# Staging and splitting the weights of a seven-product matmul two quarters at a time

## The chip, the cores and the metric

The kernel runs on one core of one Trainium2 chip. The metric is the device time of one execution in microseconds, median of several. Before the change it is 1718.91 us (three runs, 1718.07 to 1722.91).

## The reference

Two layers of a hybrid decoder trunk on 512 tokens of width 2048, all in float32. Each layer normalises its input, projects it through one combined matrix `w_in`, feeds three groups of heads, and projects their concatenation through `w_out` into the residual stream:

```python
def _layer(x, norm_g, w_in, ...):
    proj = _rmsnorm(x, norm_g) @ w_in        # 2048 x 7696
    # split: conv h,b,c,g (512 each); stick-breaking q,k,v,g (1024 each);
    #        linear attention q,k (256 each), v,g (512 each), low-rank gate (16)
    y_conv = _short_conv(...) * silu(cv_g)
    y_sb   = _stick_breaking(rmsnorm(q), rmsnorm(k), v) * silu(sb_g)   # 8 heads of 128
    y_gla  = _rmsnorm(_gla(...)) * silu(gl_g)                          # 4 heads
    return x + concat(y_conv, y_sb, y_gla) @ w_out                     # 2048 x 2048
```

The stick-breaking weights of a query are, strictly causally, sigmoid(z) times the product of sigmoid(-z) over the later keys; the kernel forms them by a scan backwards over a row of scores.

## The kernel before

**Projections.** Both matrices are worked through in groups of 256 columns: 26 of `w_in` and 8 of `w_out` in each layer. A group's 2 MB of float32 weights are fetched into one of two staging tiles `st` (`fetch`, L343). Each element is split into a high and a low float16 part (`wh`, `wl`), after scaling by a power of two that comes from the sum of the squares. A product of two such numbers takes three float16 matmuls: high by high, high by low, low by high. The scale comes from two Square instructions on ACT, one for each half of the staging tile (`wmax`, L366), a reduction over partitions on POOL (L380) and five tiny instructions on DVE (`wscale`). An ordinary group is then split in two halves of 128x2048 (L435 on ACT, L442 on DVE) and multiplied by 192 matmuls of 256 columns or 96 of 512 (`project_toks`, L683 to L685; `project_cols`, L673 to L675), or by tokens (L814).

**Quick groups.** 25 of the 68 groups take seven block products instead of eight, in the manner of Strassen and Winograd (`project_quick`, L749). These are g, k and the second "conv h" of `w_in` in each layer (18), and three and four groups of `w_out`. The 2048x256 weights are seen as quarters: r is the parity of the 128-row tile, c the half of the columns; b11, b12, b21, b22 are strided views of the staging tile. Sums of the quarters give four more blocks. `wsums` (L471) makes the sums in place and splits all seven blocks, 128x1024 each: the high part on ACT (L485), the low part on DVE (L486). The sums are four additions on DVE for `w_out` (L492 to L498), or three on DVE (L506, L508, L511) and one accumulating DMA on POOL's queue (L503). Each of the three buffers of `wh` and `wl` takes two blocks (parts 0 and 1, 2 and 3, 4 and 5), a separate tile `w7h`, `w7l` the seventh. The matching sums of the left operand lie ready (`xsums`, `msums`).

Each product is 24 matmuls of 256 columns (L764) or 48 of 128 (L767). Seven products go into four accumulators in two PSUM banks: pa and pd in one, pb and pf in the other. Between them ACT and DVE take the values out (L778 to L792): y12 from pa after the first product, y21 from pb, y22 from pd, y11 from pa after the fifth, and so on. The products stand in the order pa w11, pb wT2, pd wT3, pf w22, pa w21, pb wt1, pd wT4. A matmul with `start` clears its bank's accumulation state, so only the first product in a bank has it.

**What sets the order.** DVE's and ACT's instructions are written out by hand only up to the first projection. From there on a planner orders the instructions of every engine: it runs the program on a timeline of its own, takes at each step what its operands allow, by priority, and inserts the semaphores. Each engine then executes its list strictly in that order. The preparation of weights has high priority. `weights()` (L515), called as a group starts, issues the fetch of the group after the next, and leaves two hooks: after the first three matmuls of the running group the squares of the next group are queued, and later (after the second product of a quick group, L779) its scaling and splits. A fetch waits until its staging tile's last reader is through; the fetches, the accumulating DMA and the POOL reductions share POOL's queue.

**Attention.** Each pair of heads j has four groups v, g, q, k, so quick and ordinary groups alternate. `attend` queues two `scores` and two `values`, which run beside the next pair's projections. `scores` (L1226 for the matmuls) computes the scores of four query tiles in two chunks, as `CHUNKS` (L40) lists them: tiles 3 and 2, then 0 and 1, with their column offsets in PSUM. Then come two sigmoids, a scan, a product, the split into float16 (L1244, L1245) and DMA transposes from SP's queue into `th`. The transposes of q and k (`qT`, `kT` from `qp`) go through the same queue. `values` multiplies by the values (L1263) into a single bank, whose two halves DVE evicts by two instructions (L1270).

Of the kernel before, what the change touches and what calls it, by code (L numbers as in the profile page):

```python
# [6 lines left out]
F16 = mybir.dt.float16  # L7
# [3 lines left out]
AF = mybir.ActivationFunctionType  # L11
ALU = mybir.AluOpType
# [5 lines left out]
P = 128  # L18
# [18 lines left out]
TWICE = ("wm", "wgm", "wq", "ws", "wp", "vu", "bm", "bsmix", "gsmix", "lr", "xr0", "xrm", "xrt", "xtot", "xrstd", "xrs")  # L37


CHUNKS = ((((3, 0), (2, 512)), (3, 2)), (((0, 0), (1, 128)), (0, 1)))  # L40


@with_exitstack
def hybrid_trunk(ctx, tc, x, norm_g, w_in, conv_w, conv_b, sb_qn_g, sb_kn_g,
# [7 lines left out]
    HK = KT // 2  # L52
# [18 lines left out]
    def nm(s):  # L71
        uid[0] += 1
        return f"{s}_{uid[0]}"
# [4 lines left out]
    def wk(shape, tag, bufs=None, dt=F32):  # L78
        return work.tile(shape, dt, tag=tag, name=nm(tag), bufs=bufs)
# [266 lines left out]
    def fetch(i):  # L346

        l, src, cols = specs[i]
        queue = nc.gpsimd if i > 2 else nc.sync
        staged[i] = st = []  # L350
        whole[i] = stage.tile([P, KT, GW], F32, tag="st", name=nm("st"))
        for h in range(2):
            s_ = whole[i][:, h * HK:(h + 1) * HK, :]
            c0 = cols[0][0]
            queue.dma_start(s_, src[l, h * HK * P:(h + 1) * HK * P, c0:c0 + GW].rearrange("(k p) n -> p k n", p=P))  # L355
# [110 lines left out]
    def hook(mm):  # L466

        if hooks:
            hooks.pop(0)(mm)

    def wsums(i):  # L471

        sc = scales[i]
        b11, b12, b21, b22 = (whole[i][:, r::2, c * P:(c + 1) * P] for r in range(2) for c in range(2))
        parts = loaded[i][0]
        for _ in range(3):
            a = [wpool.tile([P, HK, GX], F16, tag=t, name=nm(t)).rearrange("p k c -> p (k c)") for t in ("wh", "wl")]
            parts.extend([p_[:, n * HK * P:(n + 1) * HK * P] for p_ in a] for n in range(2))
        parts.append([wk([P, HK * P], t, 1, dt=F16) for t in ("w7h", "w7l")])
        for n in range(7):  # L480
            parts[n] = [a.rearrange("p (k c) -> p k c", c=P) for a in parts[n]]

        def split(b, n):
            h_, l_ = parts[n]
            hi = S.activation(h_, b, AF.Copy, scale=sc)  # L485
            V.scalar_tensor_tensor(l_, b, sc, h_, ALU.mult, ALU.subtract)  # L486
            return hi


        if specs[i][1] is w_out:  # L490
            split(b11, 0)
            V.tensor_tensor(b11, b11, b12, ALU.add)  # L492
            split(b22, 3)
            V.tensor_tensor(b12, b12, b22, ALU.add)
            V.tensor_tensor(b22, b11, b22, ALU.add)
            split(b22, 1)
            split(b12, 2)
            V.tensor_tensor(b22, b22, b21, ALU.add)  # L498
            split(b21, 4)
            split(b11, 5)  # L500
            split(b22, 6)
            return
        G.dma_start(out=b12, in_=b11, accum_op=ALU.add)  # L503
        split(b11, 0)
        split(b22, 3)
        V.tensor_tensor(b22, b12, b22, ALU.add)  # L506
        split(b22, 1)
        V.tensor_tensor(b11, b22, b11, ALU.subtract)  # L508
        split(b11, 2)
        split(b21, 4)  # L510
        V.tensor_tensor(b21, b22, b21, ALU.add)  # L511
        split(b12, 5)
        split(b21, 6)

    def weights():  # L515

        i = cursor[0]
        cursor[0] += 1
        if i + 2 < len(specs):
            with tc.high_priority():  # L520
                fetch(i + 2)
        assert not hooks
# [134 lines left out]
    for l in range(depth):  # L657
# [90 lines left out]

        def project_quick(src, sums, y, cols):  # L749

            (w11, wT2, wT3, w22, w21, wt1, wT4), u = weights()
            (pa, pd), (pb, pf) = ([bk[:, n * GW:(n + 1) * GW] for n in range(2)]
                                  for bk in [bank(psp, "p") for _ in range(2)])
            a11, a12, a22 = ([a[:, 2 * r:2 * r + 2, c::2, :] for a in src] for r, c in ((0, 0), (0, 1), (1, 1)))
            s_, a21_22, a12_s, a11_21 = sums

            def prod(o, w, a, start, stop=False):
                for t in range(1 if cols else 2):
                    for kk in range(HK):
                        for i, (p_, q_) in enumerate(((0, 0), (0, 1), (1, 0))):  # L760
                            st_ = start and t == kk == i == 0
                            en = stop and kk == HK - 1 and i == 2
                            if cols:
                                mm = T.matmul(o, w[q_][:, kk, :], a[p_][:, :, kk, :], start=st_, stop=en,  # L764
                                              skip_group_check=True)
                            else:
                                mm = T.matmul(o[:, t * P:(t + 1) * P], a[p_][:, t, kk, :], w[q_][:, kk, :], start=st_,  # L767
                                              stop=en, skip_group_check=True)
# [9 lines left out]
            S.activation(y12, za, AF.Copy)  # L778
            hook(prod(pb, wT2, s_, True))  # L779
            V.tensor_tensor(y21, zb, y12, ALU.subtract)  # L780
            prod(pd, wT3, a11_21, False)
            S.activation(y22, zd, AF.Copy)
            prod(pf, w22, a12_s, False)
            prod(pa, w21, a12, False)
            S.activation(y11, za, AF.Copy)
# [428 lines left out]
        def attend(j, qT, kT, vh, vl, vu, g, s_):  # L1214
# [34 lines left out]
            def values(hh):  # L1249
                hs = slice(hh * P, (hh + 1) * P)  # L1250
                op = bank(psm, "m").rearrange("p (t c) -> p t c", c=P)
                y = wk([P, NT, P], "e")
                for n, (qtiles, cols) in enumerate(CHUNKS):
                    at = {t: 7 * n + o // P for t, o in qtiles}
                    top, q0 = max(at), min(at)
                    for kt in range(top + 1):

                        ts_ = [t for t in cols if t >= kt]
                        first = at[ts_[0]] + kt
                        step = at[cols[1]] - at[cols[0]]  # L1260
                        c0 = 2 * n + cols.index(ts_[0])
                        for i, (a_, b_) in enumerate(((vh, 0), (vh, 1), (vl, 0))):
                            T.matmul(op[:, c0:c0 + len(ts_), :], a_[:, kt, hs],  # L1263
                                     th[hh][:, b_, first:first + (len(ts_) - 1) * step + 1:step, :],
                                     start=n == i == kt == 0, stop=n == 1 and i == 2 and kt == top,
                                     skip_group_check=True)
                for n, (_, cols) in enumerate(CHUNKS):
                    q0 = min(cols)
                    a = op[:, 2 * n:2 * n + 2, :]
                    V.scalar_tensor_tensor(y[:, q0:q0 + 2, :], a[:, ::-1, :] if cols[0] > cols[1] else a, vu[:, 1:2],  # L1270
                                           g[:, hh, q0 * P:(q0 + 2) * P].rearrange("p (t c) -> p t c", c=P),
                                           ALU.mult, ALU.mult)
# [158 lines left out]
```

## Time and profile before

| | |
|---|---|
| median of 3 runs | 1718.91 us |
| the profiled execution's own time | 1717.69 us |
| its span, first to last instruction | 1715.9 us |
| mean granted TensorE clock | 0.992 |
| PE, DVE, ACT, POOL busy | 97%, 78%, 66%, 14% of the span |
| DMA packets moved | 227.26 MB, mean 132 GB/s |

A row of a group reads: line, engine, operation, tile written <- tiles read, shapes, count | busy time in us, mean ns of one | idle time of the engine just before, and what ended most of it. "psp" are the PSUM banks of the projections, "st" the staging tiles, "m", "x" and "s" left operands and their sums. PE is TensorE's matmuls, PEld its weight loads, SP the queue of the transposes.

### The profile page before, as it was taken

The page shows a single profiled execution, that of the slowest core. Times are in us where ns is not written, and L with a number is a line of the kernel's source. Part 1 is how long each engine was busy: PE and PEld are TensorE (multiplying, and loading weights), DVE is VectorE, ACT ScalarE, POOL GpSimd, SP SyncE. Part 2 cuts the span into 40 slices and gives each one's busy share as a digit, 9 for nine tenths or more (in the row PEclk, how much of TensorE's full clock was granted, in tenths as well). Part 3 has the DMA queues.
Part 4 walks back from the last instruction along what each step waited for, and adds up shares of the span by engine and source line. Part 5 has one row for each costly group of instructions (what it writes and reads, how often), then busy time and mean ns, then how long its engine had stood idle before and what let it go on. Part 6 is the DMA issues. An engine that isn't in the chain of part 4 may idle for free.

```text
span 1715.9 us, 36876 instructions
## 1 busy us (share of the span) xinstructions
PE 1669.9 (97%) x15642; PEld 1298.4 (76%) x15642; DVE 1331.3 (78%) x2327; ACT 1129.1 (66%) x1619; POOL 239.2 (14%) x286
## 2 busy tenths in 40 slices
PE   7999999999999989999989999999999999899999
PEld 5644548989898964799976455689898889548998
DVE  8975889877878767785688677997786888677883
ACT  7667677767666656666665676776765767565662
POOL 1211111111111111001122101121111111101110
PEclk9999999999999999999999999999999999999999
DMA  7233323566766686245543332446666667753441
GB/s 251 83 114 98 99 64 99 145 116 152 136 149 139 147 233 164 77 150 181 186 103 108 116 102 75 118 123 125 148 136 105 146 132 150 201 153 108 162 151 50
DMA packets 181478, 227.26 MB, mean 132 GB/s; under 512 B 94194, under 2 KB 141628, under 8 KB 180800
## 3 DMA queue, kind: packets, MB, share of 16 engines
q0 software_dynamic: 60352, 168.83, 34.4%
q1 hardware_dynamic: 111952, 46.61, 14.4%
q10 hardware_dynamic: 9008, 9.45, 1.7%
q8 instruction: 122, 2.00, 0.5%
q14 instruction: 44, 0.36, 0.1%
HBM read 179.65 MB, written 14.68 MB: 113 GB/s over the span
## 4 chain that ended last, share of the span: by engine, by line
PE 73%; DVE 12%; DMA 7%; ACT 4%; issue 3%; POOL 0%; DVEq 0%; ACTq 0%
PE psp L767 13%; PE psp L674 8%; PE psp L675 8%; PE psp L673 8%; PE psp L685 7%; PE psp L684 7%; PE psp L683 7%; PE psp L814 6%; PE psp L764 3%; DMA st<-in_w_in_dram 2%; DVE wl L486 2%; DMA th<-za 2%; DMA kT<-qp 2%; ACT junk L366 1%; DVE wl L442 1%
## 5 line engine op out<-in xcount | busy, mean ns | idle before, releaser
L366 ACT ACTIVATE junk<-st 128x2048 uint8<-128x2048 f32 x150 | 285.1, 1901 | 44.1 <-DMA st<-in_w_in_dram 42.8
L442 DVE SCALAR_TENSOR_TENSOR wl<-st,ws,wh 128x2048 f16<-128x2048 f32 x102 | 239.2, 2347 | 80.7 <-ACT wh L435 80.7
L435 ACT ACTIVATE wh<-st,ws 128x2048 f16<-128x2048 f32 x100 | 199.3, 1998 | 105.4 <-PE psp L674 47.1
L684 PE MATMUL psp<-wl,m 128*128 128x256 f16 x960 | 261.7, 273 | 0.0
L683 PE MATMUL psp<-wh,m 128*128 128x256 f16 x960 | 261.7, 273 | 0.0
L685 PE MATMUL psp<-wh,m 128*128 128x256 f16 x960 | 261.7, 273 | 0.0
L485 ACT ACTIVATE wh<-st,ws 128x1024 f16<-128x1024 f32 x150 | 167.6, 1143 | 120.5 <-DVE st L506 57.7
L486 DVE SCALAR_TENSOR_TENSOR wl<-st,ws,wh 128x1024 f16<-128x1024 f32 x150 | 189.6, 1279 | 27.4 <-ACT wh L485 27.3
L355 POOL DMA_DIRECT2D st<-in_w_in_dram x114 | 102.2, 900 | 436.0 <-DVE wl L442 319.4
L683 PE MATMUL psp<-wh,x 128*128 128x256 f16 x512 | 139.6, 273 | 0.0
L684 PE MATMUL psp<-wl,x 128*128 128x256 f16 x512 | 139.6, 273 | 0.0
L685 PE MATMUL psp<-wh,x 128*128 128x256 f16 x512 | 139.6, 273 | 0.0
L675 PE MATMUL psp<-x,wl 128*128 128x512 f16 x352 | 134.4, 382 | 2.2 <-DVE zun L186 2.2
L674 PE MATMUL psp<-x,wh 128*128 128x512 f16 x352 | 134.4, 382 | 0.0
L673 PE MATMUL psp<-x,wh 128*128 128x512 f16 x352 | 134.0, 381 | 0.0
L673 PE MATMUL psp<-m,wh 128*128 128x512 f16 x352 | 133.9, 380 | 0.0
L674 PE MATMUL psp<-m,wh 128*128 128x512 f16 x352 | 133.9, 380 | 0.0
L675 PE MATMUL psp<-m,wl 128*128 128x512 f16 x352 | 133.9, 380 | 0.0
L675 PEld LDWEIGHTS <-wl 128*128 128x128 f16 x704 | 69.2, 98 | 85.0 <-DVE wl L442 2.7
L673 PEld LDWEIGHTS <-wh 128*128 128x128 f16 x704 | 69.2, 98 | 81.5 <-issue 3.1
L380 POOL PARTITION_ALL_REDUCE wgm<-wm x75 | 40.0, 533 | 648.2 <-ACT junk L366 633.6
L674 PEld LDWEIGHTS <-wh 128*128 128x128 f16 x704 | 69.2, 98 | 80.8 <-issue 2.3
(427 smaller groups left out, 4042.2 us busy)
## 6 DMA issues: line engine op xcount, KB each, us to landing
st<-in_w_in_dram POOLq DMA_DIRECT2D x114, 1024.0 KB, 8.4
st<-in_w_out_dram POOLq DMA_DIRECT2D x32, 1024.0 KB, 7.4
st<-st POOLq DMA_DIRECT2D x18, 512.0 KB, 8.3
st<-in_w_in_dram SPq DMA_DIRECT2D x6, 1024.0 KB, 12.0
mixd<-g POOLq DMA_DIRECT2D x24, 256.0 KB, 7.7
x<-in_x_dram SPq DMA_DIRECT2D x4, 1024.0 KB, 4.9
qT<-in_x_dram ACTq DMA_DIRECT2D x8, 512.0 KB, 3.8
qT<-xs ACTq DMA_DIRECT2D x8, 512.0 KB, 3.9
```

Source lines behind the costliest of these rows:

```text
L366: sq = S.activation(junk(HK * GW).rearrange("p (k n) -> p k n", k=HK), staged[i][h], AF.Square, accum_out=peak[i][:, h:h + 1])
L435: hi = S.activation(wh[:, :, :GW], staged[i][h], AF.Copy, scale=scales[i])
L442: V.scalar_tensor_tensor(wl[:, :, :GW], staged[i][h], scales[i], wh[:, :, :GW], ALU.mult, ALU.subtract)
L485: hi = S.activation(h_, b, AF.Copy, scale=sc)
L486: V.scalar_tensor_tensor(l_, b, sc, h_, ALU.mult, ALU.subtract)
L673: T.matmul(o, wh[:, kk, cs], xh[:, :, k, :], start=st_, stop=False)
L674: T.matmul(o, wh[:, kk, cs], xl[:, :, k, :], start=False, stop=False)
L675: mm = T.matmul(o, wl[:, kk, cs], xh[:, :, k, :], start=False, stop=en)
L683: T.matmul(o, ah[:, t, k, :], wh[:, kk, :n], start=st_, stop=False, skip_group_check=True)
L684: T.matmul(o, ah[:, t, k, :], wl[:, kk, :n], start=False, stop=False, skip_group_check=True)
L685: return T.matmul(o, al[:, t, k, :], wh[:, kk, :n], start=False, stop=en, skip_group_check=True)
L767: mm = T.matmul(o[:, t * P:(t + 1) * P], a[p_][:, t, kk, :], w[q_][:, kk, :], start=st_, stop=en, skip_group_check=True)
```

## The change

Three things are changed.

*Staging.* A quick group's weights are fetched by three DMAs instead of two, so that in each pair of row tiles the quarters lie side by side as b22, b11, b12, b21, 128 columns each. The first DMA brings b22 (512 KB in rows of 512 bytes), the second b11 and b12 (1 MB in rows of 1 KB), the third b21 (512 KB in rows of 512 bytes). The two Squares read columns 0 to 255 and 256 to 511 of that layout.

*Splits and products.* `wsums` splits b22 and b11 by one instruction on each engine, forms the sums in place, splits the two results by one, b12 and b21 by one, and the last sum alone. The same seven blocks come out, in the order w22, w11, wT2, wT3, wt1, w21, wT4. The sums of `w_out` groups are formed by the same formulas as those of `w_in`, with the first addition on DVE. The products now stand in the order pa w11, pf w22, pb wT2, pd wT3, pa w21, pb wt1, pd wT4, and the second hook stands after pf's product.

*Values.* The second chunk holds tile 1 at column 0 and tile 0 at column 256, so the four tiles lie in the bank in the order 3, 2, 1, 0, and one instruction of 128x512 evicts them, reading backwards by tiles.

```diff
-CHUNKS = ((((3, 0), (2, 512)), (3, 2)), (((0, 0), (1, 128)), (0, 1)))
+CHUNKS = ((((3, 0), (2, 512)), (3, 2)), (((1, 0), (0, 256)), (1, 0)))
...
+        if i in quick:
+            w = src[l, :, c0:c0 + GW].rearrange("(k r p) n -> p r k n", p=P, r=2)
+            own = whole[i].rearrange("p (k r) c -> p k (r c)", r=2)
+            for o, r, c in ((0, 1, slice(P, GW)), (P, 0, slice(0, GW)), (P + GW, 1, slice(0, P))):
+                queue.dma_start(own[:, :, o:o + c.stop - c.start], w[:, r, :, c])
+            st.extend(own[:, :, h * GW:(h + 1) * GW] for h in range(2))
+            return
...
+        own = whole[i].rearrange("p (k r) c -> p k (r c)", r=2)
+        b22, b11, b12, b21 = (own[:, :, n * P:(n + 1) * P] for n in range(4))
...
+        def split(src):
+            n = src.shape[2] // P
+            if n == 1:
+                pair = [wk([P, HK * P], t, 1, dt=F16) for t in ("w7h", "w7l")]
+            else:
+                pair = [wpool.tile([P, HK, GX], F16, tag=t, name=nm(t)).rearrange("p k c -> p (k c)")[:, :HK * n * P]
+                        for t in ("wh", "wl")]
+            h_, l_ = (a.rearrange("p (k c) -> p k c", c=n * P) for a in pair)
+            S.activation(h_, src, AF.Copy, scale=sc)
+            V.scalar_tensor_tensor(l_, src, sc, h_, ALU.mult, ALU.subtract)
+            parts.extend([a[:, :, m * P:(m + 1) * P] for a in (h_, l_)] for m in range(n))
...
         if specs[i][1] is w_out:
+            V.tensor_tensor(b12, b12, b11, ALU.add)
+        else:
+            G.dma_start(out=b12, in_=b11, accum_op=ALU.add)
+        split(own[:, :, :2 * P])
         V.tensor_tensor(b22, b12, b22, ALU.add)
-        split(b22, 1)
         V.tensor_tensor(b11, b22, b11, ALU.subtract)
-        split(b11, 2)
-        split(b21, 4)
+        split(own[:, :, :2 * P])
+        split(own[:, :, 2 * P:])
         V.tensor_tensor(b21, b22, b21, ALU.add)
-        split(b12, 5)
-        split(b21, 6)
+        split(b21)
...
-            (w11, wT2, wT3, w22, w21, wt1, wT4), u = weights()
+            (w22, w11, wT2, wT3, wt1, w21, wT4), u = weights()
...
-            hook(prod(pb, wT2, s_, True))
+            hook(prod(pf, w22, a12_s, True))
+            prod(pb, wT2, s_, False)
             V.tensor_tensor(y21, zb, y12, ALU.subtract)
             prod(pd, wT3, a11_21, False)
             S.activation(y22, zd, AF.Copy)
-            prod(pf, w22, a12_s, False)
             prod(pa, w21, a12, False)
...
-                for n, (_, cols) in enumerate(CHUNKS):
-                    q0 = min(cols)
-                    a = op[:, 2 * n:2 * n + 2, :]
-                    V.scalar_tensor_tensor(y[:, q0:q0 + 2, :], a[:, ::-1, :] if cols[0] > cols[1] else a, vu[:, 1:2],
-                                           g[:, hh, q0 * P:(q0 + 2) * P].rearrange("p (t c) -> p t c", c=P),
-                                           ALU.mult, ALU.mult)
+                V.scalar_tensor_tensor(y, op[:, ::-1, :], vu[:, 1:2], g[:, hh, :].rearrange("p (t c) -> p t c", c=P),
+                                       ALU.mult, ALU.mult)
```

More of the change, by code (lines that the diff above doesn't have):

```diff
@@ L351, in fetch @@
         whole[i] = stage.tile([P, KT, GW], F32, tag="st", name=nm("st"))
+        c0 = cols[0][0]
+        if i in quick:
[5 more added lines that the diff above has]
+            return
         for h in range(2):
             s_ = whole[i][:, h * HK:(h + 1) * HK, :]
-            c0 = cols[0][0]
             queue.dma_start(s_, src[l, h * HK * P:(h + 1) * HK * P, c0:c0 + GW].rearrange("(k p) n -> p k n", p=P))
@@ L473, in wsums @@
         sc = scales[i]
-        b11, b12, b21, b22 = (whole[i][:, r::2, c * P:(c + 1) * P] for r in range(2) for c in range(2))
+        own = whole[i].rearrange("p (k r) c -> p k (r c)", r=2)
+        b22, b11, b12, b21 = (own[:, :, n * P:(n + 1) * P] for n in range(4))
         parts = loaded[i][0]
-        for _ in range(3):
-            a = [wpool.tile([P, HK, GX], F16, tag=t, name=nm(t)).rearrange("p k c -> p (k c)") for t in ("wh", "wl")]
-            parts.extend([p_[:, n * HK * P:(n + 1) * HK * P] for p_ in a] for n in range(2))
@@ L479, in wsums @@
[L479 to L487, printed above, removed]
-        if specs[i][1] is w_out:
[L491 to L495, printed above, removed]
-            split(b22, 1)
-            split(b12, 2)
-            V.tensor_tensor(b22, b22, b21, ALU.add)
-            split(b21, 4)
-            split(b11, 5)
-            split(b22, 6)
-            return
@@ L503, in wsums @@
-        G.dma_start(out=b12, in_=b11, accum_op=ALU.add)
-        split(b11, 0)
-        split(b22, 3)
+        def split(src):
[9 more added lines that the diff above has]
+            parts.extend([a[:, :, m * P:(m + 1) * P] for a in (h_, l_)] for m in range(n))
```

2 lines of the change are left out of this document (removed).

## The prediction

> **What bounds the kernel now.** I read the page's head first, then the waits of TensorE, then the stages, then the lines that the diff touches.
>
> ```profile
> span 1715.9 us, 36876 instructions
> PE 1669.9 (97%) x15642; PEld 1298.4 (76%) x15642; DVE 1331.3 (78%) x2327; ACT 1129.1 (66%) x1619; POOL 239.2 (14%) x286
> PE 73%; DVE 12%; DMA 7%; ACT 4%; issue 3%; POOL 0%; DVEq 0%; ACTq 0%
> ```
>
> TensorE is busy 1669.9 of 1715.9 us, and the diff leaves its number of matmuls and their shapes as they are. So the change can win only where TensorE waits, and lose wherever it makes TensorE wait. The waits of PE, longest first (engine and line that waits, what ended it, us in total, times, longest):
>
> ```profile
> PE psz L1226 <- DMA kT<-qp: 11.0, 2, 5.9
> PE psp L764 <- ACT g L785: 5.5, 6, 1.9
> PE psp L814 <- DMA m<-raw: 4.9, 1, 4.9
> ...
> PE psm L1263 <- DVE e L1270: 3.6, 1, 3.6
> ...
> PE psp L767 <- DVE wl L486: 1.3, 1, 1.3
> ...
> PE psp L764 <- DVE wl L486: 1.0, 2, 0.6
> ...
> PE psp L764 <- ACT qT L778: 0.6, 2, 0.3
> ...
> PE psp L764 <- DVE g L780: 0.2, 1, 0.2
> ```
>
> What touches seven-product groups directly is 5.5 + 1.3 + 1.0 + 0.6 + 0.2 = 8.6 us, half a per cent of the run. Another 11.0 + 3.6 lie in attention stages which the engines that prepare weights make late. The 4.9 at L814 belongs to the change of layers and isn't touched. The stages (us, then busy time of PE, PEld, DVE, ACT, POOL, clock, DMA share, GB/s):
>
> ```profile
> 455.00:540.00 85.00, 84.73 (x945) 77.32 (x943) 69.97 (x125) 59.05 (x94) 14.41 (x16) 1.00 0.65 147
> 540.00:640.00 100.00, 92.96 (x970) 79.71 (x968) 77.10 (x136) 68.23 (x104) 16.59 (x19) 0.99 0.67 160
> 1300.00:1393.00 93.00, 87.40 (x946) 79.07 (x944) 69.85 (x125) 59.59 (x94) 14.39 (x16) 0.98 0.69 134
> 1393.00:1492.00 99.00, 91.82 (x963) 79.00 (x961) 76.99 (x136) 67.51 (x104) 16.55 (x19) 1.00 0.72 161
> 1616.00:1692.00 76.00, 76.00 (x1351) 75.63 (x1349) 62.84 (x82) 46.63 (x51) 6.94 (x10) 1.00 0.42 137
> ```
>
> The middle of a layer (455 to 540) and the last four quick groups (1616 to 1692) are full. The loss is in 540:640 and 1300:1492, some 20 us of PE, with DVE at 75 to 78% and DMA at two thirds.
>
> **Part 1, splitting two quarters at a time.** (us busy, mean ns. These count six parts of each of 25 groups; the seventh, w7, is as long.)
>
> ```profile
> L442 DVE SCALAR_TENSOR_TENSOR wl<-st,ws,wh 128x2048 f16<-128x2048 f32 x102 | 239.2, 2347 | 80.7 <-ACT wh L435 80.7
> L435 ACT ACTIVATE wh<-st,ws 128x2048 f16<-128x2048 f32 x100 | 199.3, 1998 | 105.4 <-PE psp L674 47.1
> L485 ACT ACTIVATE wh<-st,ws 128x1024 f16<-128x1024 f32 x150 | 167.6, 1143 | 120.5 <-DVE st L506 57.7
> L486 DVE SCALAR_TENSOR_TENSOR wl<-st,ws,wh 128x1024 f16<-128x1024 f32 x150 | 189.6, 1279 | 27.4 <-ACT wh L485 27.3
> ```
>
> Now a group takes seven splits: ACT 7 x 1.143 = 8.00 us, DVE 7 x 1.279 = 8.95. After it takes three of double width and one single: ACT 3 x 1.998 + 1.143 = 7.14, DVE 3 x 2.347 + 1.279 = 8.32. Over 25 groups that frees 21.6 us of ACT and 15.8 of DVE. Beside a full PE this is worth nothing by itself. What counts is the order: the first split now holds both untouched quarters, and products one and two read exactly these. The sums wait for one split instead of two in different buffers, and the third product's weights, late before (1.3 at L767, in the wait list), get a product more of slack. I take the 1.3 + 1.0 of weight waits as gone: **-2.3**. Bounds: -2.3 to +2.5, since each double split also delivers its first half up to 1.998 - 1.143 + 2.347 - 1.279 = 1.9 us later. That is covered by PE's work on the group before. The cover is short only where TensorE waited for L486 already, three places, so I set +2.5 as an estimate for the upper end.
>
> On the chain through 540:640 and 1393:1492 (DVE in a row, then the transposes of k) two quick groups are prepared in each stage. Each is shorter by 0.63 us of DVE, and I add as much again for hand-offs between the engines that go: 2 x 2 x 0.65 = **-2.6** off the 11.0. Bounds 0 (the DMA queue decides alone) and -11.0.
>
> **Part 2, the products in another order.** Two accumulators share a PSUM bank: pa with pd, pb with pf. How long is a product? From the chain of waits:
>
> ```profile
> 1300.37 5.24 PE psp L764 x48
> ```
>
> 48 matmuls of two products take 5.24, so a product is 2.6 us. And what does the next one in the same bank wait for? ACT's timeline (start, us, what):
>
> ```profile
> 387.79 1.91 ACT L366 ACTIVATE junk<-st 128x2048 uint8<-128x2048 f32 x1 [4.56 <-DMA st<-in_w_in_dram]
> 389.60 0.19 ACT L366 ACTIVATION_READ_ACCUMULATOR junk<-st 128x1 f32 x1
> 389.69 0.36 ACT L785 ACTIVATE g<-psp 128x256 f32<-128x256 f32 x1
> ```
>
> and TensorE's:
>
> ```profile
> 390.11 0.27 PE L764 MATMUL psp<-x,w7h 128*128 128x256 f16 x1 [1.06 <-ACT g L785]
> ```
>
> At 390.11 the seventh product, which writes pd, starts 0.06 us after L785 has read pa: other columns, same bank. Turns in a bank are therefore taken whole. Before, pa, pd, pa, pd stood one product apart each time. After, the order is pa, pf, pb, pd, pa, pb, pd. The first turn gets two products of slack, so the 0.6 at L778 and the 0.2 at L780 go: **-0.8**. But the fifth product (pa) now follows the fourth (pd) directly, with L782 between them.
>
> The Trainium skill, "PSUM — Partial Sum Buffer", section "PSUM bank collisions raise a hardware error", says to guard PSUM by bank and quadrant, not by address, and so speaks against this order: every fifth product would wait for the eviction. The trace agrees at 390.11.
>
> The price of that turn (the product after L782's begins, then L782):
>
> ```profile
> 1624.04 0.22 PE L767 MATMUL psp<-wh,th 128*128 128x128 f16 x1
> ```
>
> ```profile
> 1624.23 0.39 ACT L782 ACTIVATE g<-psp 128x256 f32<-128x256 f32 x1 [1.53 <-PE psp L767]
> ```
>
> What covers it, from the groups of lines in the stretch 608.2 to 619.2:
>
> ```profile
> L764 PE MATMUL psp<-s,wh 128*128 128x256 f16 x62 | 10.5, 273 | 0.3 <-ACT qT L778 0.3
> L764 PE MATMUL psp<-s,wl 128*128 128x256 f16 x31 | 8.5, 273 | 0.3 <-DVE wl L486 0.3
> ```
>
> With ACT idle the eviction ends at 1624.62, 0.58 us after the next product began; uncovered, 25 x 0.6 = 15 us. The cover: ahead of the fifth product, 62 + 31 = 93 matmuls read the sums "s", though products two to four have only 3 x 24 = 72. The planner had put 21 of the sixth product there to bridge this very eviction. The sixth writes the other bank, so it can fill the gap again. I take **+1.0** (25 x 0.04); bounds 0 and +15.
>
> **Part 3, three DMAs for two.** (KB each, median us to landing.)
>
> ```profile
> st<-in_w_in_dram POOLq DMA_DIRECT2D x114, 1024.0 KB, 8.4
> st<-st POOLq DMA_DIRECT2D x18, 512.0 KB, 8.3
> ```
>
> The issues (mean ns of one):
>
> ```profile
> L355 POOL DMA_DIRECT2D st<-in_w_in_dram x114 | 102.2, 900 | 436.0 <-DVE wl L442 319.4
> L503 POOL DMA_DIRECT2D st<-st x18 | 28.8, 1599 | 3.2 <-issue 2.1
> ```
>
> One quick group's fetch, on POOL, and the second square that waits for it, on ACT:
>
> ```profile
> 380.95 1.81 POOL L355 DMA_DIRECT2D st<-in_w_in_dram  x2 [7.62 <-DVE w7l L486]
> ```
>
> ```profile
> 391.06 1.91 ACT L366 ACTIVATE junk<-st 128x2048 uint8<-128x2048 f32 x1 [1.00 <-DMA st<-in_w_in_dram]
> ```
>
> 2 MB as before, but 1 MB of it in rows of 512 bytes into strided places. The nearest rows for such an issue are 0.90 us (plain) and 1.60 (512-byte pieces, accumulating). POOL issues for 2.7 to 4.8 us instead of 1.8; the reduction of the next weights and the accumulating DMA queue behind it, at 14% load. The first square used to need one megabyte, at 387.79 in this example, the second the other, at 391.06: 3.3 us per MB. Now the first needs pieces one and two, 1.5 MB: 1.6 us later. Behind the squares on ACT stands L785, and behind that the seventh product: the 5.5 us above. Here the planner decides. If the eviction goes ahead of the square, which is ready later, the 5.5 go; if not, six waits grow by 1.6 each, +9.6. I take half of the gain, **-2.8**.
>
> The Trainium skill, "DMA: Bandwidth & Descriptors", section "Rules for kernel authors", asks for at least 1 MiB per DMA; with the fixed 2.0 us of its section "Anatomy of one DMA" the third piece would cost 2 us of staging (estimate). The trace doesn't bear that out clearly: its 512 KB land at 8.3 as 1 MB does at 8.4.
>
> **Part 4, one eviction per head.** Two evictions of 128x256 at L1270 become one of 128x512. The pair, and the nearest row for the one:
>
> ```profile
> 611.69 0.87 DVE L1270 SCALAR_TENSOR_TENSOR e<-psm,vu,g 128x256 f32<-128x256 f32 x2
> 372.98 0.68 DVE L1287 SCALAR_TENSOR_TENSOR v<-psp,v 128x512 f16<-128x512 f32 x1
> ```
>
> 16 x 0.19 = 3 us of DVE, hidden behind PE: 0. The 3.6 us at L1263 is DVE being late, not long; bounds -3.6 and 0.
>
> **Sum.** -2.3 - 2.6 - 0.8 + 1.0 - 2.8 = -7.5 us. The profiled execution took 1717.7 (span 1715.9 and 1.8 around it); so 1710.2 there. The median shown, 1718.9, is 1.2 above it: **1711**, with its own range 1706 to 1714.
>
> **Rivals.**
> *Nothing shows.* PE is at 97%, and the freed 37 us of ACT and DVE lie under it; DMA sets the 11.0. Against it: four kinds of wait belong to code that is rewritten. 1714 to 1724.
>
> *The square holds the eviction (slower).* ACT takes its instructions in order; the quick group's first square waits for 1.5 MB, L785 stands behind it, the seventh product behind L785. It decides once the plan leaves L785 behind the square at most of the six places. Then +9.6, the third piece's issue (0.9 to 1.6, six times) up to +9.6 more where its square comes first, and the weight waits gone: 1718.9 + 9.6 - 3.1 = 1725, up to 1735. For it: the 4.56 us of idle ACT at 387.79 and 42.8 us of such idling in all:
>
> ```profile
> L366 ACT ACTIVATE junk<-st 128x2048 uint8<-128x2048 f32 x150 | 285.1, 1901 | 44.1 <-DMA st<-in_w_in_dram 42.8
> ```
>
> Against it: 540:640 and 1393:1492 would absorb their part in the wait for k.
>
> *The bank turn isn't bridged (slower).* +15 - 3.1: 1731. For it: the last four groups have nothing else to run. Against it: the 21 matmuls above.
>
> **Chances.** Forecast 0.42 (in it 0.08 for the whole 11.0 or more, below 1706), nothing shows 0.27, square 0.20, bank turn 0.11. About 0.3%, 5 us, is what a measurement here can tell from no change. Faster by more: 0.42; within: 0.27; slower by more: 0.31. The range, 1702 to 1730, leaves out the end of the bank turn and of the square, and the largest gains.
>
> **What would show it.** Right: no wait for the split's line at L764 or L767, L785's wait below 3 us, kT's below 9. Fill matmuls of the sixth product ahead of the fifth, and no wait for L782's successor. Wrong: PE waiting at the fifth product for an ACT eviction, 25 times; longer idling of ACT before L366; the waits for kT or th grown, which would say that the DMA engines pay for the shorter rows. The planner orders all engines anew, which no row shows; a new wait of 5 us in attention would overturn the sum in either direction.

## The result and the profile after

The changed kernel takes 1777.05 us (median of 4 runs, 1774.12 to 1785.68) against 1718.49 for the kernel before on the same chip: ratio 1.0349 with a 95% interval of 1.0304 to 1.0394, some 58 us slower. The forecast was 1711, the range 1702 to 1730. The time lies above both, and above both rivals that end slower. A layer has 30 groups of `w_in`, not 26, so the groups are 76 in all and not 68; the 25 quick ones are as counted. Line numbers of the changed kernel: evictions y12 L773, y21 L776, y22 L778, y11 L780; quick matmuls L759 and L762; splits L494 (ACT) and L495 (DVE); squares L373; sums L503, L504, L507; a head's first sigmoid L1229, high part of its products L1239.

The head of the page and the chain:

```profile
span 1773.8 us, 36791 instructions
PE 1681.8 (95%) x15642; PEld 1304.8 (74%) x15642; DVE 1314.2 (74%) x2236; ACT 1111.4 (63%) x1544; POOL 264.4 (15%) x311
PE 26%; DVE 9%; DMA 8%; ACT 7%; issue 4%; POOL 1%; ACTq 0%; POOLq 0%; DVEq 0%
```

DVE and ACT work 17 us less each, about as the prediction worked out, and the kernel is slower. Span less PE's busy time is TensorE's idle time: 46.0 us before, 92.0 now. That is 46 of the 58 us; the other 12 are in PE's busy time, for the same matmuls. Where? The stretch from the first k to the last k of a layer's attention, then the last four quick groups, before:

```profile
327.50:605.50 278.00, 276.00 (x3183) 252.42 (x3181) 222.93 (x403) 192.87 (x308) 46.53 (x51) 1.00 0.65 143
1171.20:1458.00 286.80, 278.18 (x3183) 253.90 (x3181) 223.15 (x403) 193.04 (x308) 45.82 (x51) 0.99 0.70 138
```

and after (the last row answers to 1616 to 1692):

```profile
329.80:640.60 310.80, 282.92 (x3184) 255.59 (x3183) 217.19 (x379) 186.56 (x285) 51.01 (x59) 0.98 0.60 127
1211.30:1520.60 309.30, 285.40 (x3185) 258.57 (x3183) 217.00 (x379) 186.99 (x285) 51.01 (x59) 0.97 0.60 128
1673.70:1749.70 76.00, 75.82 (x1327) 75.26 (x1325) 62.58 (x72) 45.01 (x42) 11.27 (x12) 1.00 0.44 137
```

Attention lost 32.8 us in the first layer and 22.5 in the second, 55 of 58. The last four groups, made of nothing but the rewritten code, are as full as before. So neither the splits nor the products nor the bank turns are slow as such; what is late are the groups between which scores and normalisations run. The four largest waits of PE over the whole span (engine, line and what ended the wait: us in total, times, longest):

```profile
PE psp L762 <- ACT kT L773: 18.9, 6, 3.4
PE psp L762 <- ACT raw L1305: 8.9, 4, 2.7
PE psp L762 <- ACT kT L780: 7.7, 5, 2.6
PE psz L1221 <- DMA kT<-qp: 7.3, 5, 2.5
```

Three of four are evictions of PSUM by ACT, which is busy 63% of the time. Waits of ACT and DVE that ended at a DMA:

```profile
ACT junk L373 <- DMA st<-in_w_in_dram: 68.1, 24, 6.2
ACT za L1229 <- DMA th<-za: 56.3, 10, 10.6
DVE st L503 <- DMA st<-st: 26.8, 9, 6.8
```

Before, ACT's waits of za for the score transposes th<-za were:

```profile
ACT za L1234 <- DMA th<-za: 12.0, 5, 4.2
```

One such wait in the changed kernel, on ACT, with what followed:

```profile
388.12 0.95 ACT L1239 ACTIVATE za<-zw 128x896 f16<-128x896 f32 x1
...
392.38 1.91 ACT L373 ACTIVATE junk<-st 128x2048 uint8<-128x2048 f32 x1 [2.62 <-DMA st<-in_w_in_dram]
...
396.32 0.36 ACT L780 ACTIVATE g<-psp 128x256 f32<-128x256 f32 x1
407.32 1.01 ACT L1229 ACTIVATE za<-psz,nzun 128x896 f32<-128x896 f32 x1 [10.63 <-DMA th<-za]
...
422.22 2.00 ACT L494 ACTIVATE wh<-st,ws 128x2048 f16<-128x2048 f32 x1 [5.80 <-DVE pmix L186]
424.13 0.58 ACT L1305 ACTIVATE raw<-psp 128x512 f32<-128x512 f32 x1
```

The second head's sigmoid (407.32) needs a za buffer that the first head's transposes still read. ACT takes its list in order and stands 10.63 us, and DVE, whose scan needs that sigmoid, stands 12.82:

```profile
408.36 2.07 DVE L1234 TENSOR_TENSOR_SCAN za<-za,ones 128x512 f32<-128x512 f32 x2 [12.82 <-ACT za L1229]
```

q's eviction (424.13) comes later in ACT's list, and PE waits 2.72 us for it. ACT's wait of 5.80 us for DVE lies between, so how much of the 2.72 is due to the sigmoid isn't shown. The same place before:

```profile
377.85 0.97 ACT L1244 ACTIVATE za<-zw 128x896 f16<-128x896 f32 x1
...
392.97 0.99 ACT L1234 ACTIVATE za<-psz,nzun 128x896 f32<-128x896 f32 x1
```

There 15.1 us lie between the copy and the sigmoid, filled by a split, two squares, small evictions and waits for the squares' fetch, and the transposes are done by then. After, the fetch of the squares' data went out 4.7 us ahead of the copy, where it followed it by 3.1 before (380.95 in the prediction):

```profile
383.39 2.68 POOL L357 DMA_DIRECT2D st<-in_w_in_dram  x3 [4.03 <-DVE w7l L495]
```

So the squares are over at 396.3, and ACT reaches the sigmoid 8.6 us after the copy. The other half is the landing of this head's transposes, after and then before:

```profile
DMA to landing us min/median/max: 4.0/8.8/13.6
```

```profile
DMA to landing us min/median/max: 7.8/8.8/9.8
```

Each view has two landings, so its median is only their mean. The one that ACT waits for, of the low part, was issued at 393.6, took 13.6 us and landed at 407.2; before, it was issued at 383.9, took 7.8 and was there 1.3 us ahead of the sigmoid. In this place ACT came 6.5 us sooner after the copy (8.6 for 15.1) and the transpose took 5.8 us longer: each is about half of the wait. Why it took longer isn't shown; over the whole kernel the median landing of th<-za is 3.6 us, against 4.3 before.

### The profile page after: what moved, and what is told of

Read it like the earlier page. It is cut to its first block, busy times and chain, and to the rows that moved or that the text cites. A ratio compares the mean times of both kernels' runs of the same rounds, so it can differ in the third digit from the quotient of the medians.

```text
span 1773.8 us, 36791 instructions
## 1 busy us (share of the span) xinstructions
PE 1681.8 (95%) x15642; PEld 1304.8 (74%) x15642; DVE 1314.2 (74%) x2236; ACT 1111.4 (63%) x1544; POOL 264.4 (15%) x311
## 4 chain that ended last, share of the span: by engine, by line
PE 26%; DVE 9%; DMA 8%; ACT 7%; issue 4%; POOL 1%; ACTq 0%; POOLq 0%; DVEq 0%
PE psp L762 4%; PE psp L670 4%; PE psp L669 4%; PE psp L668 4%; PE psp L809 3%; DMA st<-in_w_in_dram 3%; ACT wh L494 2%; ACT junk L373 2%; DMA st<-st 2%; PE psp L680 2%; PE psp L679 2%; PE psp L678 2%; DMA th<-za 1%; DVE wl L449 1%; DVE wl L495 1%
## 5 line engine op out<-in xcount | busy, mean ns | idle before, releaser
L373 ACT ACTIVATE junk<-st 128x2048 uint8<-128x2048 f32 x150 | 285.3, 1902 | 75.3 <-DMA st<-in_w_in_dram 68.1
L449 DVE SCALAR_TENSOR_TENSOR wl<-st,ws,wh 128x2048 f16<-128x2048 f32 x102 | 239.1, 2347 | 59.5 <-ACT wh L442 59.3
L442 ACT ACTIVATE wh<-st,ws 128x2048 f16<-128x2048 f32 x100 | 198.1, 1997 | 64.5 <-DVE ws L403 30.0
L495 DVE SCALAR_TENSOR_TENSOR wl<-st,ws,wh 128x2048 f16<-128x2048 f32 x75 | 176.0, 2349 | 72.2 <-ACT wh L494 72.0
L494 ACT ACTIVATE wh<-st,ws 128x2048 f16<-128x2048 f32 x75 | 149.1, 1994 | 105.1 <-DVE qrt L216 52.9
L387 POOL PARTITION_ALL_REDUCE wgm<-wm x75 | 43.9, 585 | 710.3 <-ACT junk L373 696.6
L762 PE MATMUL psp<-wh,s 128*128 128x128 f16 x1024 | 94.1, 225 | 29.4 <-ACT kT L773 18.9
```

The costliest lines, as they stand in the source:

```text
L373: sq = S.activation(junk(HK * GW).rearrange("p (k n) -> p k n", k=HK), staged[i][h], AF.Square, accum_out=peak[i][:, h:h + 1])
L442: hi = S.activation(wh[:, :, :GW], staged[i][h], AF.Copy, scale=scales[i])
L449: V.scalar_tensor_tensor(wl[:, :, :GW], staged[i][h], scales[i], wh[:, :, :GW], ALU.mult, ALU.subtract)
L494: S.activation(h_, src, AF.Copy, scale=sc)
L495: V.scalar_tensor_tensor(l_, src, sc, h_, ALU.mult, ALU.subtract)
```

## The experiments

Theories as they stood at first: **A**, DVE takes the sums, which wait for the accumulating DMA, ahead of k's normalisation, so k and the scores come late; **B**, the third DMA delays squares and accumulation; **C**, the product order; **D**, only the combination is slow. All ratios are to the kernel before, run beside each kernel on the same chip. Code excerpts are shortened, and some lines stand in words for the edit.

### Taking one part out of the changed kernel

Two fetches of 1 MB (quarters in the order b21, b22, b11, b12; the last pair split singly):

```
-    for o, r, c in ((0, 1, slice(P, GW)), (P, 0, slice(0, GW)), (P + GW, 1, slice(0, P))):
+    for n, r in enumerate((1, 0)):
```

> The changed kernel with its staging by two DMAs of 1 MB in rows of 1 KB (the layout b21, b22, b11, b12; b12 and b21 are then split singly, 128x1024 each). Theory A (the sums go ahead: with one double split before them they are planned in front of k's normalisation on DVE, which then stands at the accumulating DMA): 1765 to 1785, L503 still waits for the accumulating DMA by 15 us or more. Theory B (the third DMA and the rows of 512 bytes make the squares and the accumulation late): 1735 or less, ACT's wait for st back from 68 to about 43 us. Theory C (order of the products): 1765 to 1785.

The old product order:

```
-    hook(prod(pf, w22, a12_s, True)); prod(pb, wT2, s_, False)
+    hook(prod(pb, wT2, s_, True))            # and pf again after pd
```

> The changed kernel with the products in the order of before (pa w11, pb wT2, pd wT3, pf w22, pa w21, pb wt1, pd wT4). Theory C (the new order makes the fourth product wait for y12 and the fifth for y22): 1735 or less, the 18.9 us of the wait for L773 gone. Theories A and B: 1765 to 1785, the waits for late evictions of ACT stay at other products.

The old seven splits with their old sequence of sums:

```
-    split(own[:, :, :2 * P])
+    split(b11, 0); split(b22, 3)             # and so on, as before
```

> The changed kernel with seven single splits in the order of before (b11, b22, then the sums), but the new staging, the new order of products and the one eviction. Theory A: 1730 or less, since two splits in two buffers stand before the sums again, and k's normalisation is planned ahead of them; DVE's wait for the accumulating DMA below 5 us. Theories B and C: 1760 to 1785.

Measured: 1.0089 (1.0067 to 1.0110), 1.0187 (1.0155 to 1.0219), 1.0084 (1.0056 to 1.0112). Each gives back a large part, 28 to 46 us of 58, so the effects do not add. The first run has the time that B expected, and neither B's nor A's wait left with it:

```profile
ACT junk L373 <- DMA st<-in_w_in_dram: 68.6, 27, 5.3
DVE st L505 <- DMA st<-st: 18.5, 9, 4.1
```

So these two waits don't set the time by themselves. The second run lies between what C and what A and B expected, the third comes near A's 1730. With the old order PE waits at the fourth eviction instead:

```profile
PE psp L759 <- ACT g L780: 32.9, 6, 11.7
```

### Adding one part to the kernel before

The eviction of a head's values alone:

> The kernel before with the one eviction and the new second chunk alone. All three theories: 1712 to 1724. If it is at 1740 or more, the values' part or the replanning that any edit brings is the cause.

The three DMAs alone, the order alone, the double splits alone (two fetches, two double splits, three single ones):

> The kernel before with the staging by three DMAs alone (single splits, products in the order of before, two evictions). Theory B (the first square needs 1.5 MB, and y11's eviction stands behind it on ACT): 1726 to 1740, the wait for y11 (5.5 us in six before) at 15 or more. Theory A (sums ahead of k's normalisation): 1714 to 1722, nothing in the order of DVE has changed. Theory D (only the three parts together are slow): 1714 to 1724.

> The kernel before with the products in the new order alone. Theory C (the new order costs by itself, since pd and pa follow each other in one bank): 1735 or more, waits of PE for y12 and y22 that sum to 15 us or more. Theories A, B and D: 1712 to 1724.

> The kernel before with the double splits alone: two DMAs of 1 MB in the layout b21, b22, b11, b12, two double and three single splits, the order of products of before. Theory A: 1728 to 1745, DVE's wait for the accumulating DMA 10 us or more. Theories B, C and D: 1712 to 1724.

| part added to the kernel before | ratio | 95% interval |
|---|---|---|
| eviction | 1.0014 | 0.9990 to 1.0037 |
| product order | 0.9978 | 0.9956 to 1.0000 |
| three DMAs | 1.0104 | 1.0047 to 1.0162 |
| double splits | 1.0229 | 1.0175 to 1.0283 |
| all (the change) | 1.0349 | 1.0304 to 1.0394 |

C falls as a cause by itself: alone the order costs nothing. D falls too: the three DMAs and the double splits are each slow alone, and the four differences add up to 3.25%, near the 3.49% of all. (This sum is no rule: order and eviction together, added to the double splits, are the first run above, 1.0089 against 1.0229.) The three DMAs land in B's range of 1726 to 1740, but ACT waits 42.1 us for st, as before (42.8), so B's mechanism isn't seen. The double splits cost most. They come with the new sequence of sums. In that kernel one row of PE's waits holds 29.4 us:

```profile
PE psp L763 <- ACT g L784: 29.4, 6, 10.3
```

It is y11, and ACT's list shows why, here at the longest of the six, where PE waits 10.34 us until 586.71: the eviction stands behind a sigmoid that waits for the transposes.

```profile
584.48 1.01 ACT L1233 ACTIVATE za<-psz,nzun 128x896 f32<-128x896 f32 x1 [7.08 <-DMA th<-za]
585.38 1.00 ACT L1235 ACTIVATE zw<-psz,zun 128x896 f32<-128x896 f32 x1
586.27 0.38 ACT L784 ACTIVATE g<-psp 128x256 f32<-128x256 f32 x1
```

The accumulating DMA replaced by DVE's addition, in the changed kernel:

```
-            G.dma_start(out=b12, in_=b11, accum_op=ALU.add)
+            V.tensor_tensor(b12, b12, b11, ALU.add)
```

> The changed kernel with the first sum of the w_in groups formed by DVE too, so that no accumulating DMA is left (18 more additions of 1.22 us on DVE, 22 us in all, and 18 DMAs less). Theory A: 1758 or less, since the 26.8 us for which DVE stands at L503 go, and with them part of the lateness of k. Theories B and C: 1770 or more, as DVE only gets more work.

1.0200 (1.0136 to 1.0263): about 25 us back. That fitted A, so A was tried directly.

### Mending the order of the lists

In the changed kernel an order without a semaphore puts the sums behind k's low part; in the kernel with the double splits alone, one puts the second head's sigmoids behind y11; the third run has both in the changed kernel:

```
+    order(sum_of_b22, last low part of k)    # L503 behind L1328
+    order(first sigmoid of head 1, last y11)
```

> The changed kernel with one order added: on DVE the sums of a w_in group stand behind the low part of k that was emitted last (L503 behind L1328); nothing is left out. In the changed kernel L503 stood 2.96 us at the accumulating DMA at 362.48 with k's normalisation behind it, and k's low part ran at 372.67 against 357.84 in the kernel before. Theory A (the sums planned ahead of k's normalisation are the largest part of the loss): at least 25 of the 58 us come back, 1720 to 1750 us, DVE's waits of st<-st (26.8 us) go to under 10 and ACT's waits of za for th<-za (56.3 us) to under 30. Rival B (the late landing of the third DMA and of the accumulation is the loss, wherever the sums stand): DVE's wait goes, ACT's split L494 still waits as long, and the time stays at 1760 or over. Rival D (the two evictions y12 and q's raw stand behind the splits of double length, whatever k does): PE's waits for kT L773 (18.9 us) and raw L1305 (8.9 us) stay, 1755 to 1775.

> The kernel with the double splits alone (1.0229), and one order added: the sigmoids of a pair's second head (L1233 there) stand behind the gate's fourth eviction y11 on ACT; nothing is left out. Theory E (in that kernel PE's 29.4 us for g<-L784 are y11 standing behind a sigmoid that waits for th<-za): that wait goes to under 8 us and 20 to 30 of the 39 us come back, 1720 to 1737 us. Rival F (the transposes landing behind the fetches hold the scores themselves, so PE waits the same time for scores or values): the wait moves to psz or th and the time stays within 10 us of 1755.

> The changed kernel with both orders (sums behind k's low part, second head's sigmoids behind y11); nothing is left out. If the two inversions are independent and both stand in the changed kernel's list once the first is mended, 5 to 20 us under the run with the first order alone; if the first order brings the transposes back in time, the sigmoid no longer waits and the two runs are within 3 us. Rival B: no order helps, 1760 or over.

Measured: 1.0389 (1.0350 to 1.0429), 1.0227 (1.0196 to 1.0257), 1.0390 (1.0357 to 1.0423). Nothing came back: the first and third compare with 1.0349, the second with 1.0229. With the sums behind k, k's low part ran at 365.14 instead of 372.67:

```profile
365.14 1.23 DVE L1328 SCALAR_TENSOR_TENSOR qp<-kT,qp 128x1024 f16<-128x1024 f32 x1 [1.12 <-ACT qp L1327]
366.29 1.22 DVE L503 TENSOR_TENSOR st<-st 128x1024 f32<-128x1024 f32 x1
```

but ACT stood longer at the transposes, and y11 behind it:

```profile
PE psp L759 <- ACT g L780: 49.7, 8, 11.2
```

```profile
ACT za L1229 <- DMA th<-za: 73.5, 8, 15.0
```

**Theory A falls** as the main cause, although DVE's wait for the accumulating DMA went only from 26.8 to 17.1 us here; a later run takes 40 us of it away, and the time stays there too. In the kernel with double splits alone, y11 ahead of the sigmoids (second run) took its wait from 29.4 to 10.8, and the time moved to other rows:

```profile
PE psp L763 <- ACT g L784: 10.8, 6, 3.0
PE psm L1262 <- DVE e L1269: 9.4, 5, 2.2
```

What all these kernels keep is ACT's wait at th<-za, 39 to 74 us where y11 or the sums were moved. Theory **G** therefore: the want of a free za buffer. The seventeen kernels that use za as before, the two of the change and some that come below among them, bear it out as far as rows can. The wait for the score transposes is 3 to 17 us in the six kernels with ratios up to 1.0089, 21 to 39 in five of the six from 1.0104 to 1.0229 (the old order, 58.6, is the exception), and 47 to 74 in the five above. That the two go together does not say which brings which.

### Taking that wait away

The second chunk of a head's scores keeps its products beside its sigmoids in a zw buffer, so the two za buffers are left to the two heads:

```
-    a = wk([P, 896], "za")                   # both chunks
-    w = wk([P, zw], "zw")
+    # chunk 0 as before; chunk 1:
+    w = wk([P, 1024], "zw"); a, w = w[:, zw:2 * zw], w[:, :zw]
```

> The changed kernel, but the second chunk of a head's scores (384 columns) keeps its products beside its sigmoids in a buffer of tag zw instead of one of the two za buffers, so that the second head's first sigmoid no longer waits for the transposes of the first head's first chunk; nothing is left out. Theory G (ACT standing at the score transposes, 56.3 us in the changed kernel, 73.5 with the sums behind k, holds the evictions): that wait goes to under 15 us and the time to 1725 to 1755. Rival I (ACT and DVE hand work to and fro in longer pieces and are late everywhere; the transposes are only where the lateness shows): the wait moves to another line and the time stays within 12 us of 1777.

> The version with the new product order and the one eviction (0.9938), with the second chunk's products in the zw buffer as in the run on the changed kernel; nothing is left out. In that version ACT waits for th<-za 3.5 us and PE for kT<-qp 0.5 us, so theory G says that nothing is to be had: within 0.3% of 1705. Over 1712 if the buffer itself costs something (the second chunk waits for a zw buffer), which would then also be in the run on the changed kernel.

In the changed kernel 1.0147 (1.0120 to 1.0173), 35 us back. ACT's wait for the score transposes went from 56.3 us to 0.4, and another wait for a za buffer, 11.2 us at L906, went too. The sigmoid now follows at once:

```profile
390.10 0.54 ACT L1239 ACTIVATE zw<-zw 128x384 f16<-128x384 f32 x1
391.26 1.01 ACT L1229 ACTIVATE za<-psz,nzun 128x896 f32<-128x896 f32 x1 [0.62 <-DVE psz L1225]
```

and y12's wait fell from 18.9 to

```profile
PE psp L762 <- ACT kT L773: 6.9, 3, 3.4
```

The control is the fastest version (below), where ACT waits only 3.5 us for the score transposes and 8.9 at the other place (L911): 0.9910 (0.9892 to 0.9927) with the buffer, 0.9938 (0.9917 to 0.9959) without, some 5 us by ratios whose intervals overlap. G holds for the larger part of the loss, as far as one run and its control go. The buffer also lets the lists be planned anew, and other edits that do so gave back as much, so not every one of the 35 us is proved to be the wait itself. With the wait gone, 1.5% stays.

With the buffer, DVE stands longer at the accumulating DMA, 59.0 us; A was tried once more on top of it:

```profile
DVE st L503 <- DMA st<-st: 59.0, 15, 8.6
```

> The changed kernel with the second chunk's products in the zw buffer (1.0147) and the sums behind k's low part besides; nothing is left out. With the buffer alone DVE stands 59.0 us in 15 waits at the accumulating DMA before L503. Theory A, left over (those waits hold k and the scores, once ACT no longer stands at the transposes): DVE's wait goes under 25 us and 10 to 25 us come back, 1717 to 1732. Rival (those waits lie beside PE's work, as in the run with the sums behind k alone): within 8 us of 1742.

The wait went down,

```profile
DVE st L503 <- DMA st<-st: 19.3, 8, 3.6
```

and the time did not: 1.0170 (1.0119 to 1.0221). Those 40 us lay beside PE's work.

### What in the double splits

```
+    S.activation twice on 128x1024 in place of once on 128x2048    # high parts
+    V.scalar_tensor_tensor twice in place of once                  # low parts
```

> The changed kernel with the high parts of the double splits made on ACT by two instructions of 128x1024 and the low parts on DVE by one of 128x2048; nothing is left out. Single splits throughout gave back 43 of the 58 us. Theory I1 (an eviction stands behind a piece of 2.0 us on ACT that cannot be parted): 25 to 43 us come back, 1735 to 1752. Theory I2 (the low part of 2.35 us on DVE and what waits for all of it is the cost): under 12 us come back, 1765 or over.

> The changed kernel with the high parts of the double splits on ACT by one instruction of 128x2048 and the low parts on DVE by two of 128x1024; nothing is left out. Theory I1 (the piece of 2.0 us on ACT): under 12 us come back, 1765 or over. Theory I2 (the low part on DVE): 25 to 43 us, 1735 to 1752. If each half alone gives back 10 to 25, the cost is the hand-over itself (low part after the whole high part, 2.0 then 2.35 us, where the singles overlap by pieces).

> The changed kernel with every double split made of four instructions (two high parts of 128x1024 on ACT, then two low parts on DVE), in the changed kernel's own sequence of splits and sums; nothing is left out. Parting the high parts alone or the low parts alone gave nothing back (1.0375, 1.0314), the old seven splits in their old sequence gave 43 us. Theory S (it is the sequence, both sums between the first pair of splits and the second, that makes the parts late, not the width of an instruction): 1765 to 1780. Rival W (width: only when neither engine has a piece of 2 us does the hand-over overlap): 1730 to 1750.

High parts parted: 1.0375 (1.0326 to 1.0425), nothing back. Low parts parted: 1.0314 (1.0284 to 1.0344), some 6 us. Both: 1.0215 (1.0171 to 1.0260). So no single piece of 2 us holds the evictions. Both together give back 23 us, and the old sequence of sums, with its own formulas for `w_out`, another 23 (1.0084). Neither S nor W is confirmed: on this one path each has about half.

### The fastest version

The kernel before with the new order and the one eviction, old staging, old splits:

> The kernel before with the new product order and the eviction of a head's values by one instruction, old staging and old single splits; nothing is left out. The two alone measured 0.9978 [0.9956, 1.0] and 1.0014 [0.999, 1.0037]. If they add: 0.999, within 0.3% of the kernel before. If the order of products alone opens a gain that the eviction does not touch: 0.996 to 0.999, a version faster than both. If the lists of the engines are planned anew by the eviction and an inversion appears: 1.005 or over.

0.9938 (0.9917 to 0.9959), 1704.94 us against 1714.33: faster than both kernels, more than the two alone would give. With the second chunk in the zw buffer 1702.71 against 1718.00. TensorE is idle 35.4 us of the span in the first of them:

```profile
span 1702.3 us, 36846 instructions
PE 1666.9 (98%) x15642; PEld 1296.5 (76%) x15642; DVE 1328.9 (78%) x2311; ACT 1128.2 (66%) x1619; POOL 243.0 (14%) x286
```

## Why the prediction was wrong

**The step that failed** is in part 1: "That is covered by PE's work on the group before", with +2.5 as the upper end. The later delivery of a double split was priced by PE's waits for the weights themselves (L486). For the rewritten splits those did stay small, 4.2 us in two rows after, 2.3 before, within the bound. But the splits are steps in the lists of ACT and DVE, and the same lists hold the evictions, k's normalisation and the scores. Alone the double splits, with the new sequence of sums that comes with them, cost 2.29%, 39 us (30 to 49), and PE's wait for one eviction, y11, went from 5.5 to 29.4 us. That row is where the lateness showed, not its source: with y11 moved ahead it fell to 10.8 and the time stayed.

**The freed time** (21.6 us of ACT, 15.8 of DVE by the prediction; 17.7 and 17.1 by the two pages, with the eviction) was rightly priced at nothing. It didn't make the kernel safe: in the place shown ACT came to the second head's sigmoid 6.5 us sooner after the copy and stood there. The rows put that down to the fetch that went out earlier (383.39); what the freed time had to do with it isn't shown. The -2.6 for k's wait had the right row: kT<-qp went from 11.0 to 7.3 us. It was outweighed.

**Part 2** was right alone. The order measured 0.9978 against a forecast of +0.2 us, and its rival at 1731 didn't come: even in the changed kernel PE waits only 1.7 us for y22, the eviction of that bank turn. The other turn went wrong there. y12, given two products of slack, 5.2 us, is the longest wait of the changed kernel, 18.9 us, which ACT takes out late (it stood idle only 1.0 us ahead of these evictions). Taking the order out of the changed kernel gave back 28 us.

**Part 3** had the wrong sign: -2.8 forecast, about +18 (8 to 28) measured alone. Its rival, the square that holds y11, gave 1725 to 1735, and the run with the staging alone, 1731, is in there; but that run shows no wait for y11 among PE's largest. What grew there were the waits for kT<-qp (13.7 us, 11.0 before) and for the eviction of the values (6.6, 3.6 before). The price was near by luck, the mechanism not.

**Part 4** was right alone (1.0014).

**The last sentence** of the prediction, that a new wait of 5 us in attention would overturn the sum, named what happened, and it stood there without a chance or a price. The row for it was in sight: ACT's 12.0 us at th<-za, in a place where a low part on DVE and a transpose that took 7.8 us to land fitted with 1.3 us to spare into the 15 us between two of ACT's instructions. The prediction treated the lists as fixed and moved single instructions in them.

**What stays open.** With the buffer the changed kernel is still 1.5% above the kernel before. Three DMAs and double splits cost 1.5% each on top of the fastest version (1.0084 and 1.0089 against 0.9938) and 4.1% together. The accumulating DMA has a share (1.0200 without it), though DVE's wait for it has none that was found. No run separates the landing of the pieces, or of the transposes, from the new lists that come with every edit.

## What to carry to other kernels

When every engine works off a list in order, look for the instructions that wait for a DMA and ask which PSUM evictions stand behind them: a buffer that is freed only by a landing transfer shouldn't be the next thing that the evicting engine needs. Here 17 us of work were saved on each of two engines and 58 us of the run were lost, so price the wait, not the work. Put each part on the kernel by itself, and take each out of the whole: here the order was worth -0.2% alone and +1.6% in the changed kernel, and with the eviction it took 1.4% off the double splits. The version to keep was two parts of four.

## What the runs showed of the hardware

A wait costs TensorE more than its length. In the kernel before, after the 5.87 us at 640.15, matmuls of 512 columns start 0.43 us apart, and from 645.3 on 0.22:

```profile
644.47 0.63 PE L674 MATMUL psp<-x,wh 128*128 128x512 f16 x1
644.90 0.59 PE L675 MATMUL psp<-x,wl 128*128 128x512 f16 x1
645.32 0.38 PE L673 MATMUL psp<-x,wh 128*128 128x512 f16 x1
645.54 0.38 PE L674 MATMUL psp<-x,wh 128*128 128x512 f16 x1
```

The Trainium skill, "TensorE: Matmul & The Clock Gate", section "Part 1: The HAM clock gate (the "warmup" mystery)", has the clock change by free-running windows of some 3.4 us, back to full rate after a busy one. The trace agrees: the granted clock of 0.81 over 636 to 640 and of 0.84 over 645 to 646 put the half rate at 638.5 to 645.3, 6.8 us or two windows, the second of them full of matmuls; the matmuls saw the last 5.2. In the changed kernel the same effect is part of the 12 us by which PE's busy time grew: the mean granted clock went from 0.992 to 0.988, which over the two spans is some 7 us more of clock withheld (estimate), and that of the two attention stretches from 1.00 and 0.99 to 0.98 and 0.97.

Half the bytes, fetched in rows of 512 bytes, landed little sooner: in a median of 6.9 us for 512 KB against 8.2 for 1 MB (8.4 before). The issue of a piece cost what it did before, 902 ns as the mean of the three (L357) and 900 before, so the prediction's lower bound of 2.7 us for three was the right one.

```profile
st<-in_w_in_dram POOLq DMA_DIRECT2D x96, 1024.0 KB, 8.2
st<-in_w_in_dram POOLq DMA_DIRECT2D x36, 512.0 KB, 6.9
```
